# Six PSUM tiles of one bank in place of three tiles of two banks, for the sums of w_down and of the embedding's gate

## The chip, the core and the metric

The kernel runs on one core of one Trainium2 chip. The metric is the device time of one execution in microseconds (us), the median of several runs. TensorE multiplies matrices into PSUM, VectorE, ScalarE and GpSimd do the elementwise work, and SyncE issues the transfers.

## What is computed

One layer of a streaming encoder for 1024 prompt rows and 128 decoding rows (1152 together), model width 1024. Two mixers (sparse attention, gated delta rule) and a merge come first; the change lies in what follows them:

```python
h2 = _rmsnorm(x, norm_ffn)
u_gate, u_val = jnp.split(h2 @ w_up, [D_FF], axis=-1)        # D_FF = 2816
...
act = jax.nn.gelu(_causal_dwconv(ext_f, conv_ffn), approximate=True)
x = x + (act * u_val) @ w_down

gate_p = jax.nn.sigmoid(_rmsnorm(x, norm_ple) @ w_ple_gate)
x = x + gate_p * (p @ w_ple)
...
y = _rmsnorm(x, norm_final)
```

All of it is in float32 and everything is kept transposed: 128 channels on the partitions, rows of x along the free dimension.

## The kernel before

**Products.** Each operand is split into a high part and a low rest (`H`, `L` for activations, `wh`, `wl` for weights; ScalarE casts the high part, VectorE or GpSimd subtracts it for the rest). A product of two 128-wide pieces is three matmuls into one PSUM sum: `wh` with `H`, `wh` with `L`, `wl` with `H`. A weight tile that lies in the buffer `T3` is named `T3H` in the trace, whether high or low.

**The stretch at issue.** The 1152 rows are three blocks `b` of 384. For each block the kernel computes w_down, then the embedding's gate, for eight output tiles `d` of 128 channels. A sum of w_down runs over 22 pieces. It is made in three parts of 8, 8 and 6 pieces, for four `d` at a time (all four first parts, then the second, then the last), so four sums are open at once and they finish one after the other at the end of the group. A sum of the gate runs over 8 pieces in one go. A sum has 384 float32 columns and takes one PSUM bank of 512.

**Evacuation.** When a sum is complete, `evac_down` has VectorE read it out of PSUM, multiplied by the norm's factors (`gt<-up,R` in the trace), add it to the residual (`B<-B,gt`), and form the gate's operand for this `d` (ScalarE `H`, VectorE `L`). `evac_pg` reads the gate's sum in the same way (`gt<-up,R`), then applies the tanh on ScalarE (`gt<-gt`) and adds the result to the residual. A bank is given back to the list of free ones after the read.

**The banks.** Before w_down come the products of w_up, whose sums are two banks wide: three tiles `up0`, `up1`, `up2` of [128, 2, 512]. Two more banks (`rp`) serve the norms. In the last products of w_up, `more_accs` takes each of the three tiles when it comes free and hands its two halves on, as the places of sums of w_down and the gate:

```python
self.accs = _Views([x[:, i, :BW] for x in self.ups.views for i in range(2)])
```

The place that has been free longest is taken first. So two sums that follow each other mostly lie in the two halves of one tile.

**The order.** The order of each engine's instructions is fixed when the program is built: a driver runs the threads of the kernel (products, evacuations, loads, weights) against a small table of costs and issues each instruction as its turn comes. The waits between engines are then put in by the framework, from the tiles that the instructions read and write. Each engine works its list off in order.

Of the kernel before, what the change touches and what calls it, by code (L numbers as in the profile page):

```python
# [7 lines left out]
F32 = mybir.dt.float32  # L8
# [8 lines left out]
PSUM = bass.MemoryType.PSUM  # L17
# [4 lines left out]
NB, BW = 3, 384  # L22
# [65 lines left out]
class _Driver:  # L88
# [23 lines left out]
    def set(self, ev):  # L112
        ev.t = self.cur.t
# [178 lines left out]
class _Kernel:  # L292
# [105 lines left out]

    def more_accs(self):

        for _ in range(3):
            x = yield self.ups
            i = 2 * next(i for i in range(3) if self.ups.views[i] is x)
            self.accs.free += [(self.drv.cur.t, i), (self.drv.cur.t, i + 1)]

    def landed(self, j, t):
        self.drv.cur.dma = t
# [2440 lines left out]
    def merge_ffn(self):  # L2848
        drv, tc = self.drv, self.tc
        base = ExitStack()  # L2850
        self.rp = self.pool(base, "rms")
        self.rpb = _Banks(self.pool(base, "rpp", space=PSUM, side="right"), [128, 512], "rp", 2)
        self.ssq = self.rp.tile([128, T], F32, name="ssq")
        self.R2 = self.rp.tile([128, T], F32, name="R2")
        self.xs = _Banks(self.rp, [128, BW], "xs", 4)
        self.sqs = _Banks(self.rp, [128, BW], "sqs", 2)
        mix = ExitStack()
        mp = self.pool(mix, "mix")
        self.MH = mp.tile([128, KD, T], F32R, name="MH")
        self.ML = mp.tile([128, KD, T], F32R, name="ML")  # L2860
        with ExitStack() as st:
            self.tgs = _Banks(self.pool(st, "tg"), [128, BW], "tg", 6)
            drv.run(drv.spawn(self.dense(self.ja), 9), self.jbd)
        self.sh.close()
        self.evst.close()
        self.acc0.free = []
        h2 = ExitStack()
        self.hp = hp = self.pool(h2, "h2", side="right")
        q = lambda n: hp.tile([128, 4, 2, 288], F32R, name=n)
        self.B1H, self.B1L = q("B1H"), q("B1L")  # L2870
        self.B2 = hp.tile([128, 2, 4, 2, 576], F32R, name="B2")
        self.B2H, self.B2L = self.B2[:, 0], self.B2[:, 1]

        self.TR = {t: hp.tile([128, 4, 2, 288], F32, name="T%d" % t) for t in (0, 2, 3)}
        self.TH, self.TL = {1: q("T1H")}, {1: q("T1L")}
        self.hev2.t = 0.0
        up0, up1 = ExitStack(), ExitStack()
        p = self.pool(up0, "up0", space=PSUM, side="right")
        self.ups = _Views([p.tile([128, 2, 512], F32, name="up0"), None, None])
        self.ups.free = self.ups.free[:1]  # L2880
        drv.spawn(self.dense(self.jo), 9)
        drv.spawn(self.dense(self.ju), 9, self.jo[-1].done)
        drv.run(self.jo[-1].done)
        mix.close()
        t13 = ExitStack()
        p = self.pool(t13, "t13")
        for t in (2, 0, 3):
            self.TH[t] = p.tile([128, 4, 2, 288], F32R, name="T%dH" % t)
        self.TL[2] = p.tile([128, 4, 2, 288], F32R, name="T2L")
        with ExitStack() as st:  # L2890
            self.fp = fp = self.pool(st, "ff")
            self.exts = _Banks(fp, [128, 1026 + 144], "fe", 2)
            self.cs = _Views([])
            self.vs = _Banks(fp, [128, T], "fv", 2)
            self.fev.t = 0.0
            for n, t in enumerate((2, 0, 3)):
                drv.spawn(self.up_parts(t), 1 + n)
            drv.run(*self.aout)
            self.pst.close()
            p = self.pool(up1, "up", space=PSUM)  # L2900
            for i in (1, 2):
                self.ups.views[i] = p.tile([128, 2, 512], F32, name="up%d" % i)
                self.ups.free.append((0.0, i))
            self.accs = _Views([x[:, i, :BW] for x in self.ups.views for i in range(2)])
            self.accs.free = []
            ends = drv.spawn(self.dense(self.jd), 9, self.ju[21].done[S4Y])
            drv.spawn(self.down_loads(), 1)
            for i in range(4):
                drv.spawn(self.load_up(0, range(i, 22, 4)), 1)
            drv.run(self.ast[21])  # L2910
        with ExitStack() as st:
            self.plev.t = 0.0
            self.wp2 = p = self.pool(st, "pl")
            self.gts = _Banks(p, [128, BW], "gt", 4)
            self.pps = _Banks(p, [128, BW], "pp", 4)
            t = self.hp.tile([128, 6, BW], F32, name="T3")
            self.araws = _Views([t[:, i] for i in range(6)])
            self.ends = []
            for b in (1, 2):
                for i in range(6):  # L2920
                    drv.spawn(self.load_up(b, range(i, 22, 6)), 2)
            drv.run(ends)
            drv.run(*self.ends)
        t13.close()
        h2.close()
        up1.close()
        up0.close()
        base.close()


# [106 lines left out]
```

## Time and profile before

| | us |
|---|---|
| median of 3 runs | 2154.72 |
| lowest and highest run | 2152.86, 2160.5 |
| the profiled execution | 2153.31 |
| its span, first to last instruction | 2151.5 |
| TensorE busy in the span | 2065.3 (96%) |
| VectorE busy | 1543.1 (72%) |
| ScalarE busy | 1001.0 (47%) |
| GpSimd busy | 838.2 (39%) |

The profile is of one execution. Its own time stands beside the runs, and its span leaves out what lies before the first and behind the last instruction. A busy time is the time in which at least one instruction of the engine is on record; matmuls overlap in it, and their ends are modelled. Every operation is recorded by one helper, so all rows have the line L192, and groups are told apart by their tiles: `up` is the tile of sums, `gt` the result of its read, `R` the norm's factors.

### The profile page before, as it was taken

The page shows a single profiled execution, that of the slowest core. Times are in us where ns is not written, and L with a number is a line of the kernel's source. Part 1 is how long each engine was busy: PE and PEld are TensorE (multiplying, and loading weights), DVE is VectorE, ACT ScalarE, POOL GpSimd, SP SyncE. Part 2 cuts the span into 40 slices and gives each one's busy share as a digit, 9 for nine tenths or more (in the row PEclk, how much of TensorE's full clock was granted, in tenths as well). Part 3 has the DMA queues.
Part 4 walks back from the last instruction along what each step waited for, and adds up shares of the span by engine and source line. Part 5 has one row for each costly group of instructions (what it writes and reads, how often), then busy time and mean ns, then how long its engine had stood idle before and what let it go on. Part 6 is the DMA issues. An engine that isn't in the chain of part 4 may idle for free.

```text
span 2151.5 us, 37608 instructions
## 1 busy us (share of the span) xinstructions
PE 2065.3 (96%) x13146; PEld 2005.0 (93%) x13146; DVE 1543.1 (72%) x3585; ACT 1001.0 (47%) x1979; POOL 838.2 (39%) x1028
## 2 busy tenths in 40 slices
PE   7999998989999999999999999999999999999997
PEld 6899988989999989999999999999999989999996
DVE  7268988888747787774354778887888866857645
ACT  5267666565535566665133433333333344335332
POOL 5344543423334444454364445565655401101101
PEclk9999999989999999999999999999999999999998
DMA  5444267676555755457764423334443486655542
GB/s 195 119 125 106 80 183 184 158 195 191 165 175 165 218 159 169 140 156 233 238 197 150 128 40 86 73 72 75 78 84 66 93 218 197 192 166 190 168 138 83
DMA packets 318156, 314.56 MB, mean 146 GB/s; under 512 B 117436, under 2 KB 277008, under 8 KB 317840
## 3 DMA queue, kind: packets, MB, share of 16 engines
q1 hardware_dynamic: 317968, 312.17, 52.2%
q8 instruction: 104, 1.70, 0.3%
q14 instruction: 84, 0.69, 0.1%
HBM read 224.91 MB, written 88.81 MB: 146 GB/s over the span
## 4 chain that ended last, share of the span: by engine, by line
PE 56%; DVE 4%; DMA 4%; issue 1%; ACT 1%; POOL 1%; SPq 1%; DVEq 0%; ACTq 0%; POOLq 0%
PE up L192 38%; PE acc L192 12%; PE at L192 6%; PE rp L192 1%; SPq L192 1%; DVE B L192 1%; DVE gt L192 1%; DVE wl L192 1%; DMA evo<-gates 1%; DMA T<-in_w_down 0%; POOL tg L192 0%; POOL wl L192 0%; DVE z L192 0%; DMA obT<-sg 0%; DMA x<-qkv 0%
## 5 line engine op out<-in xcount | busy, mean ns | idle before, releaser
L192 PE MATMUL acc<-H,wh 128*128 128x384 f32 (+2 forms) x1344 | 475.6, 354 | 6.9 <-DVE evo L192 2.1
L192 PE MATMUL acc<-L,wh 128*128 128x384 f32 (+2 forms) x1344 | 456.6, 340 | 1.8 <-POOL L L192 1.3
L192 PE MATMUL acc<-H,wl 128*128 128x384 f32 (+2 forms) x1344 | 456.6, 340 | 1.4 <-POOL wl L192 1.4
L192 POOL TENSOR_TENSOR wl<-wr,wh 128x256 fp32r<-128x256 f32 (+1 forms) x288 | 232.5, 830 | 302.0 <-ACT wh L192 285.8
L192 PEld LDWEIGHTS acc<-H,wh 128*128 128x128 f32 (+1 forms) x1344 | 253.5, 189 | 15.8 <-DVE evo L192 2.4
L192 PEld LDWEIGHTS acc<-L,wh 128*128 128x128 f32 (+1 forms) x1344 | 253.8, 189 | 6.9 <-POOL L L192 2.0
L192 PEld LDWEIGHTS acc<-H,wl 128*128 128x128 f32 (+1 forms) x1344 | 253.4, 189 | 3.6 <-POOL wl L192 2.4
L192 POOL TENSOR_TENSOR ssq<-ssq,sqs 128x384 f32<-128x384 f32 x62 | 67.9, 1094 | 406.5 <-ACT sqs L192 406.4
L192 ACT CAST wh<-wr 128x1024 fp32r<-128x1024 f32 (+3 forms) x140 | 122.5, 883 | 148.6 <-PE up L192 54.7
L192 POOL TENSOR_TENSOR wl<-s,wh 128x256 fp32r<-128x256 f32 x104 | 98.4, 964 | 145.3 <-ACT wh L192 145.3
L192 PE MATMUL up<-B,wh 128*128 128x288 f32 x704 | 143.2, 297 | 3.5 <-DVE B L192 2.8
L192 DVE SCALAR_TENSOR_TENSOR T<-fe,cwf,T 128x512 f32<-128x512 f32 x132 | 124.6, 944 | 17.8 <-ACT T L192 16.4
L192 PE MATMUL up<-T,wh 128*128 128x288 f32 (+1 forms) x416 | 125.6, 302 | 2.2 <-DVE T L192 2.2
L192 PEld LDWEIGHTS up<-B,wh 128*128 128x128 f32 x704 | 113.5, 189 | 3.9 <-DVE B L192 3.1
L192 ACT ACTIVATE ja<-SC,cola 128x768 bf16<-128x768 f32 (+2 forms) x93 | 96.7, 1039 | 37.1 <-DVE cola L192 26.8
L192 ACT CAST wh<-s 128x512 fp32r<-128x512 f32 x88 | 52.5, 620 | 122.0 <-PE up L192 122.0
L192 PE MATMUL up<-B,wl 128*128 128x288 f32 x352 | 104.4, 297 | 0.0
L192 DVE TENSOR_TENSOR wl<-wr,wh 128x512 fp32r<-128x512 f32 (+1 forms) x87 | 72.5, 849 | 29.6 <-ACT wh L192 29.6
L192 PE MATMUL up<-T2H,wh 128*128 128x288 f32 (+1 forms) x272 | 85.1, 313 | 6.4 <-DVE gt L192 3.4
L192 PE MATMUL up<-T1H,wh 128*128 128x288 f32 (+1 forms) x272 | 85.6, 315 | 0.0
L192 PE MATMUL up<-T2L,wh 128*128 128x288 f32 (+1 forms) x272 | 84.6, 311 | 0.9 <-DVE T2L L192 0.9
L192 PE MATMUL up<-T1L,wh 128*128 128x288 f32 (+1 forms) x272 | 85.1, 313 | 0.0
(483 smaller groups left out, 5991.7 us busy)
## 6 DMA issues: line engine op xcount, KB each, us to landing
wr<-in_w_in SPq DMA_DIRECT2D x48, 512.0 KB, 4.3
AT<-fv SPq DMA_DIRECT2D x22, 576.0 KB, 5.5
wr<-in_w_down SPq DMA_DIRECT2D x24, 512.0 KB, 4.2
T<-in_w_down SPq DMA_DIRECT2D x24, 512.0 KB, 3.5
wr<-in_w_up SPq DMA_DIRECT2D x22, 512.0 KB, 10.7
gates<-evo SPq DMA_DIRECT2D x48, 192.0 KB, 1.9
T<-AT SPq DMA_DIRECT2D x44, 192.0 KB, 3.8
qkv<-evo SPq DMA_DIRECT2D x36, 192.0 KB, 4.1
```

What stands on the lines that cost most here:

```text
L192: r = f(*a, **k)
```

## The change

`more_accs` no longer hands on the halves of the old tiles. When both `up1` and `up2` have come free, their pool is closed and a new one is opened with four tiles `dn0` to `dn3` of one bank each; when `up0` is free, its pool is closed for one with `dn4` and `dn5`. The sums take these six tiles as they took the six halves. Nothing else is edited.

```diff
     def more_accs(self):
 
+        got = set()
         for _ in range(3):
             x = yield self.ups
-            i = 2 * next(i for i in range(3) if self.ups.views[i] is x)
-            self.accs.free += [(self.drv.cur.t, i), (self.drv.cur.t, i + 1)]
+            got.add(next(i for i in range(3) if self.ups.views[i] is x))
+            for old, new, own, n, k in ((self.up1, self.dn1, {1, 2}, 4, {}), (self.up0, self.dn0, {0}, 2, dict(side="right"))):
+                if own <= got:
+                    old.close()
+                    got -= own
+                    p = self.pool(new, "dn%d" % n, space=PSUM, **k)
+                    for _ in range(n):
+                        i = len(self.accs.views)
+                        self.accs.views.append(p.tile([128, 512], F32, name="dn%d" % i)[:, :BW])
+                        self.accs.free.append((self.drv.cur.t, i))
...
-        up0, up1 = ExitStack(), ExitStack()
-        p = self.pool(up0, "up0", space=PSUM, side="right")
+        self.up0, self.up1, self.dn0, self.dn1 = [ExitStack() for _ in range(4)]
+        p = self.pool(self.up0, "up0", space=PSUM, side="right")
...
-            p = self.pool(up1, "up", space=PSUM)
+            p = self.pool(self.up1, "up", space=PSUM)
...
-            self.accs = _Views([x[:, i, :BW] for x in self.ups.views for i in range(2)])
-            self.accs.free = []
+            self.accs = _Views([])
...
-        up1.close()
-        up0.close()
+        self.dn1.close()
+        self.dn0.close()
```

On every engine the same instructions stand in the same order before and after, tile names aside. The waits differ, on TensorE above all. Two places follow; in brackets stands which engine's semaphore a matmul waits for (`Activation` is ScalarE).

The first place is TensorE in w_down of the first block: the last three matmuls of the sum for `d` = 0 and the first of the last part of the sum for `d` = 1, which lies in the other half of `up1`. Before:

```order
L192 MATMUL up1_14468<-T0H_14413,T3H_14414 128x384 [waits Activation_49]
L192 MATMUL up1_14468<-T2_14550,T3H_14414 128x384 [waits DVE_49]
L192 MATMUL up1_14468<-T0H_14413,T3H_14414 128x384
L192 MATMUL up1_14468<-T2H_14412,wh_20095 128x384 [waits DVE_49,Activation_49]
L192 MATMUL up1_14468<-T2L_14415,wh_20095 128x384
L192 MATMUL up1_14468<-T2H_14412,wl_20096 128x384
```

And with the change:

```order
L192 MATMUL dn0_19799<-T0H_14413,T3H_14414 128x384 [waits Activation_49]
L192 MATMUL dn0_19799<-T2_14550,T3H_14414 128x384 [waits DVE_49]
L192 MATMUL dn0_19799<-T0H_14413,T3H_14414 128x384
L192 MATMUL dn1_19800<-T2H_14412,wh_20109 128x384 [waits Activation_49]
L192 MATMUL dn1_19800<-T2L_14415,wh_20109 128x384
L192 MATMUL dn1_19800<-T2H_14412,wl_20110 128x384 [waits DVE_49]
```

The first matmul of the second sum waited for VectorE's read `gt` of the first sum, and for ScalarE's cast of its own `wh` from the buffer `wr2`; now it waits for the cast alone. The wait for `wl`, which VectorE makes before that read, stands on the matmul that uses it.

The second place is TensorE in the first block's gate: the end of one sum and the first half of the next. The read of the first sum is issued when twelve matmuls of the second have been issued. Before:

```order
L192 MATMUL up1_14468<-H3_20150,wl_20745 128x384
L192 MATMUL up1_14468<-H3_20150,T3H_14414 128x384 [waits Activation_49]
L192 MATMUL up1_14468<-L3_20151,T3H_14414 128x384
L192 MATMUL up1_14468<-H3_20150,T3H_14414 128x384 x2
...
L192 MATMUL up1_14468<-H3_20150,T3H_14414 128x384
L192 MATMUL up1_14468<-H3_20150,T3H_14414 128x384 [waits DVE_49]
L192 MATMUL up1_14468<-L3_20151,T3H_14414 128x384
```

And with the change:

```order
L192 MATMUL dn0_19799<-H3_20164,wl_20759 128x384
L192 MATMUL dn1_19800<-H3_20164,T3H_14414 128x384 [waits Activation_49]
L192 MATMUL dn1_19800<-L3_20165,T3H_14414 128x384
L192 MATMUL dn1_19800<-H3_20164,T3H_14414 128x384 [waits DVE_49]
...
L192 MATMUL dn1_19800<-H3_20164,T3H_14414 128x384 x2
L192 MATMUL dn1_19800<-L3_20165,T3H_14414 128x384
L192 MATMUL dn1_19800<-H3_20164,T3H_14414 128x384 [waits DVE_49]
```

Before, the thirteenth matmul of the second sum waited for the read, and the read for the twelfth. With the change both waits of the second sum are for low halves of its weight tile, and the read waits for the last matmul of its own sum.

## Rows read from the trace of the kernel before

**Rows 1.** The page: TensorE's busy time, and its granted clock in 40 slices.
```profile
PE 2065.3 (96%) x13146; PEld 2005.0 (93%) x13146; DVE 1543.1 (72%) x3585; ACT 1001.0 (47%) x1979; POOL 838.2 (39%) x1028
PEclk9999999989999999999999999999999999999998
```
**Rows 2.** Busy time by stretch; behind POOL the granted clock, DMA share, GB/s.
```profile
core 0: us, PE busy (x) PEld busy (x) DVE busy (x) ACT busy (x) POOL busy (x), PEclk, DMA share, GB/s
1680.00:1724.00 44.00, 44.00 (x332) 44.00 (x331) 37.81 (x57) 19.22 (x33) 18.82 (x20) 1.00 0.47 89
...
1755.00:2136.00 381.00, 361.37 (x2056) 353.65 (x2054) 244.12 (x442) 155.76 (x233) 45.17 (x41) 1.00 0.53 166
```
**Rows 3.** Waits of TensorE from 1755 us on: us in total, times, longest.
```profile
PE up L192 <- DVE gt L192: 12.0, 15, 1.4
PE up L192 <- ACT wh L192: 3.0, 4, 0.7
...
PE up L192 <- ACT T3H L192: 1.5, 2, 0.7
PE up L192 <- DVE L L192: 1.4, 3, 0.6
```
**Rows 4.** Timeline of TensorE, first block's gate: start us, us, instruction [idle before].
```profile
1840.28 0.34 PE L192 MATMUL up<-H,wl 128*128 128x384 f32 x1
1841.27 0.44 PE L192 MATMUL up<-H,wh 128*128 128x384 f32 x1 [0.65 <-DVE gt L192]
1841.56 0.33 PE L192 MATMUL up<-L,wh 128*128 128x384 f32 x1
```
**Rows 5.** Timeline of VectorE at the same place.
```profile
1840.66 0.56 DVE L192 TENSOR_TENSOR gt<-up,R 128x384 f32<-128x384 f32 x1 [0.75 <-PE up L192]
```
**Rows 6.** Timeline of TensorE, first block's w_down.
```profile
1762.26 0.34 PE L192 MATMUL up<-T0H,T3H 128*128 128x384 f32 x1
1763.34 0.41 PE L192 MATMUL up<-T2H,wh 128*128 128x384 f32 x1 [0.74 <-ACT T3H L192]
1763.59 0.33 PE L192 MATMUL up<-T2L,wh 128*128 128x384 f32 x1
```
**Rows 7.** Timeline of VectorE at the same place.
```profile
1762.63 0.56 DVE L192 TENSOR_TENSOR gt<-up,R 128x384 f32<-128x384 f32 x1 [0.47 <-PE up L192]
```
**Rows 8.** Timeline of ScalarE at the same place.
```profile
1759.34 0.83 ACT L192 CAST wh<-wr 128x768 fp32r<-128x768 f32 x1
```
**Rows 9.** Timeline of TensorE, first block, first sum of the gate.
```profile
1822.81 0.33 PE L192 MATMUL up<-L,wh 128*128 128x384 f32 x1
1822.98 0.33 PE L192 MATMUL up<-H,wl 128*128 128x384 f32 x1
1823.15 0.33 PE L192 MATMUL up<-H,wh 128*128 128x384 f32 x1
```
**Rows 10.** Timeline of TensorE, first block's w_down, two sums on.
```profile
1769.53 0.34 PE L192 MATMUL up<-T0H,wl 128*128 128x384 f32 x1
1771.24 0.41 PE L192 MATMUL up<-T2H,T3H 128*128 128x384 f32 x1 [1.38 <-DVE gt L192]
```
**Rows 11.** Timeline of VectorE at the same place.
```profile
1770.55 0.54 DVE L192 TENSOR_TENSOR gt<-up,R 128x384 f32<-128x384 f32 x1
```
**Rows 12.** Busy time in the stretch around the end of the first block's w_down.
```profile
1819.30:1827.20 7.90, 6.70 (x38) 6.38 (x38) 7.81 (x12) 5.20 (x11) 2.22 (x2) 1.00 0.33 103
```
**Rows 13.** Timeline of VectorE in that stretch.
```profile
1819.30 0.56 DVE L192 TENSOR_TENSOR gt<-up,R 128x384 f32<-128x384 f32 x1 [0.88 <-PE up L192]
...
1822.97 0.55 DVE L192 TENSOR_TENSOR gt<-up,R 128x384 f32<-128x384 f32 x1
...
1826.54 0.61 DVE L192 SCALAR_TENSOR_TENSOR L<-B,nrm,H 128x384 fp32r<-128x384 f32 x1
```
**Rows 14.** Timeline of TensorE from the seventh sum's end.
```profile
1818.39 0.34 PE L192 MATMUL up<-T0H,wl 128*128 128x384 f32 x1
...
1826.27 0.34 PE L192 MATMUL up<-H,wh 128*128 128x384 f32 x1
1827.20 0.44 PE L192 MATMUL up<-L,wh 128*128 128x384 f32 x1 [0.59 <-DVE L L192]
```
**Rows 15.** The reads of sums: duration ns min/median/max, first and last start us.
```profile
L192 DVE TENSOR_TENSOR gt<-up,R x48: 543/557/558, 1762.6 to 2134.4; 128x384 f32<-128x384 f32 x48
```

## The prediction

> **What bounds the kernel now.** I read the page first. TensorE is busy for 96% of the span and its granted clock stands at full speed in nearly every slice [rows 1], so whatever takes time from TensorE takes it from the kernel. The diff touches only the products of w_down and of the embedding's gate, so the next view is that stretch, 1755 to 2136 us: TensorE is busy 361.4 of 381.0 us there, VectorE 244.1, ScalarE 155.8, the DMA engines 53% [rows 2]. TensorE is the bound, with 19.6 us idle. Then the waits of TensorE in that stretch: 15 waits for VectorE's `gt`, 12.0 us together; 4 for ScalarE's `wh` and 2 for its `T3H`, 4.5 us; 3 for VectorE's `L`, 1.4 us [rows 3].
>
> `gt<-up,R` is VectorE's read of a finished sum out of PSUM. One of these waits, in order of time: TensorE starts the matmul before at 1840.28, the next at 1841.27 and the one behind it at 1841.56 [rows 4]. VectorE starts its read at 1840.66, for 0.56 us, and it ends just ahead of the late matmul [rows 5]. So TensorE stands still for the length of one read and the two handovers around it.
>
> The six waits put down to ScalarE are of the same kind. In the first, TensorE starts matmuls at 1762.26, 1763.34 and 1763.59 [rows 6]; a read runs from 1762.63 to 1763.19 [rows 7]; the cast that this matmul needs (`wh<-wr`, by the first place shown in the order of instructions) had ended at 1759.34 + 0.83 = 1760.17 [rows 8]. The view named the cast of a later weight tile. That makes 21 waits.
>
> **The change, part by part.** Nothing is added to the work: on all five engines the same instructions stand in the same order, tile names aside. What differs is who waits for whom. Before, two sums share a tile `up`, and the order of instructions makes the tile as a whole pass from hand to hand, though the sums lie in different banks: a matmul for the second sum that is issued behind the read of the first waits for that read. 21 matmuls have that wait before and not after, which is the count above: four in each block's w_down, three in each block's gate. In 11 of the pairs the read stands 3 to 21 matmuls deep in the second sum and before waits for those as well; after, it waits for its own sum alone.
>
> What one stall costs is the distance of matmul starts, because the ends of matmuls are modelled. Without a stall they start 0.17 to 0.18 us apart (1822.81, 1822.98 in [rows 9]); I take 0.175, so 0.35 for two steps.
> - Read deep in the next sum: 1841.56 - 1840.28 = 1.28, less 0.35 = 0.93 us [rows 4]. There are 11 of these (listed with 0.65 us idle).
> - Read right behind its sum: 1763.59 - 1762.26 = 1.33, less 0.35 = 0.98 us [rows 6]. There are 7 (listed with 0.74; six of them under ScalarE).
> - The same with VectorE still busy when the sum is ready: 1771.24 - 1769.53 = 1.71 [rows 10], plus a second step of 0.25 as in [rows 6], less 0.35 = 1.61 us. There are 3. The read itself runs 1770.55 to 1771.09 [rows 11].
>
> As a check on the counts: 11 x 0.65 + 3 x 1.38 + 0.74 = 12.0, the sum of the `gt` row in [rows 3], and six of 0.74 are 4.4 against the 4.5 of its ScalarE rows. The sum: 11 x 0.93 + 7 x 0.98 + 3 x 1.61 = 21.9 us.
>
> What is late next? All waits that stay are for weights and for the next operand. The matmul of [rows 6] would be due at 1762.26 + 0.175 = 1762.44, and its weights were there at 1760.17 [rows 8], 2.3 us earlier. The casts of later weights start when TensorE has finished an earlier weight tile, so they move forward with it. The waits that the change writes out anew, for the low halves of weights, stood before too, implied by the wait for the read, which VectorE does later than those. I cost them at nothing. No transfer is waited for either: TensorE has none in [rows 3], and the DMA engines are busy 53% [rows 2].
>
> One place gives something back: the end of w_down in each block, where the gate's last eighth of operand, `L`, comes out of the last sum's read. VectorE is busy 7.81 of 7.90 us there [rows 12], from the read of the seventh sum at 1819.30 to the end of `L` at 1826.54 + 0.61 = 1827.15 [rows 13]; 7.85 us that TensorE's speed doesn't shorten. TensorE's last matmul of that sum starts at 1818.39 [rows 14]. After, the read can start 0.38 us behind it (1840.66 - 1840.28 in [rows 4] and [rows 5]), at 1818.77, and `L` ends at 1826.62. The matmul that needs it is the 41st behind 1818.39 and would be due at 1818.39 + 41 x 0.175 = 1825.57; it waits 1.1 us, plus 0.1 for the restart. Before, it lost 1827.20 - 1826.27 - 0.175 = 0.76 [rows 14] and the same 0.1. So 0.4 us more is lost, three times: 1.2 us. Bounds for that: nothing, and the whole stall removed just ahead, 3 x 0.93 = 2.8.
>
> Reading a bank beside matmuls that write another isn't new: the 48 reads last 543 to 558 ns whether TensorE stands or runs [rows 15], and beside the read at 1822.97 [rows 13] the matmuls keep their step [rows 9]. I cost it at nothing.
>
> Gain: 21.9 - 1.2 = 20.7 us. The profiled execution took 2153.3 us, 1.8 of it around the span of 2151.5; less 20.7 is 2132.6. The median of the three runs is 1.4 above the profiled one, so I forecast 2134.
>
> **The rivals.**
> *VectorE takes over in w_down.* It is as good as full for 7.9 us at a block change [rows 12], and one stall of w_down was 1.71 long because it was busy. If all twelve waits of w_down only changed their name, each block would keep 0.98 + 1.61 + 0.98 + 0.93 = 4.5 us, 13.5 in all, and 8.4 would be gained: 2146. Against it: VectorE is busy 64% of the stretch [rows 2]. Chance 8%.
>
> *No change.* The waits could stand for real ones, for a bank that is used again, or another wait could be waiting behind each. Then the time stays at 2153 to 2155. For it: the sums lay in six banks before already. Against it: a stall comes while the second half is written and the read is of the first, and the operands were early. Chance 5%. The Trainium skill speaks for this one (Perfetto Trace Analysis, Matmuls): "Independent matmul groups should rotate through different PSUM banks so the ACT/DVE evacuation of one overlaps the next group's matmuls". By that rule the kernel before was in order and nothing would be gained; the trace disagrees, as its evacuation does not overlap, by [rows 4] and [rows 5].
>
> *Slower.* Since no engine's order changes and the waits only get fewer, it can end later only if instructions take longer. The place is the matmuls that now run beside a read. The gain is used up if the step grows by 20.7 / 2160 = 10 ns over the 2160 matmuls of both products (8 x 3 sums of 22 x 3 and 8 x 3 of 8 x 3), to 0.185 us; by 20 ns it ends 22 us slower, near 2177. Against it: the steps in [rows 9], and a stretch of 44 us with TensorE 100% busy that keeps the full clock [rows 2]. Chance 3%. The Trainium skill (PSUM — Partial Sum Buffer, PSUM bank collisions raise a hardware error) says that two engines on different banks ran clean; by that rule this rival has no price, and the trace agrees.
>
> **How the numbers follow.** The forecast has 84%. Its own ends: 21.9 gained with no offset for the median is 2131.4, and the runs of before reach 1.9 below their median, so 2129; at the top, half of the gain lost is 2153.3 - 10.4 + 1.4 = 2144. The other three cases hold 16%, so the range may end there. 0.5% of the median is 10.8 us, about what a measurement can tell from no change: faster means under 2143.9. That is the forecast and a part of the first rival, 87%; within 0.5% 10%; slower 3%.
>
> **What would show it.** Right: TensorE's row of waits for `gt` is gone, and the `wh` and `T3H` rows with it; the stretch is some 20 us shorter with about 4 us idle; reads start 0.4 us behind their own sum; the waits for `L` grow from 0.6 to about 1 us. Wrong: the same number of waits under another name (`wl`, `wh`, `L`), the step of matmuls above 0.18 us, or reads longer than 0.56 us. A lower granted clock in the stretch, or weights that land late, would also break it.

## The result, and the profile after

| | before | after |
|---|---|---|
| median of 6 runs, us | 2154.61 | 2139.44 |
| lowest and highest run | 2152.86, 2162.33 | 2132.81, 2142.96 |
| the profiled execution | 2153.31 | 2132.81 |
| its span | 2151.5 | 2131.0 |

The ratio is 0.9918 (95% interval 0.9896 to 0.994). Run again beside other kernels, with 6 runs of it and 11 of the kernel before, the changed kernel gave 0.9908 (0.9887 to 0.9929). Of the ten executions of the kernel with a tile of four banks (below), one took 3386 us at a granted clock of 0.555 and is left out of its ratio. The forecast was 2134 us, a ratio of 0.9904. The two profiled executions lie 20.5 us apart; the forecast for that was 20.7.

The page of the changed kernel, its span and its first section, beside [rows 1]:

```profile
span 2131.0 us, 37597 instructions
...
PE 2060.1 (97%) x13146; PEld 2001.8 (94%) x13146; DVE 1541.9 (72%) x3585; ACT 1000.0 (47%) x1979; POOL 842.6 (40%) x1028
```

The number of matmuls is the same; the span has lost 20.5 us, TensorE's busy time 5.2. The stretch of the two products, to the end of its matmuls, beside [rows 2]:

```profile
1755.00:2115.50 360.50, 356.82 (x2055) 354.39 (x2053) 243.74 (x441) 154.25 (x233) 47.81 (x41) 1.00 0.55 176
```

The idle time of TensorE is 3.7 us of 360.5 us here; before it was 19.6 of 381.0. Its waits from 1745 us on, beside [rows 3] (us in total, times, longest):

```profile
PE rp L192 <- ACT sqs L192: 2.7, 1, 2.7
PE rp L192 <- DVE rr_r L192: 2.4, 1, 2.4
PE dn L192 <- DVE L L192: 1.5, 3, 0.6
PE dn L192 <- ACT H L192: 1.1, 3, 0.5
PE dn L192 <- DVE T2L L192: 0.9, 1, 0.9
PE rp L192 <- POOL ssq L192: 0.8, 1, 0.8
```

The row for `gt` is gone, and the rows for `wh` and `T3H` with it: what they named was never ScalarE. (`dn` is what `up` was.) `H`, one wait of 0.2 us before, is larger and `ssq` is new; the experiments come to them. The place of [rows 6] and [rows 7], TensorE and then VectorE:

```profile
1762.05 0.34 PE L192 MATMUL dn<-T0H,T3H 128*128 128x384 f32 x1
1762.23 0.34 PE L192 MATMUL dn<-T2H,wh 128*128 128x384 f32 x1
1762.40 0.33 PE L192 MATMUL dn<-T2L,wh 128*128 128x384 f32 x1
1762.58 0.33 PE L192 MATMUL dn<-T2H,wl 128*128 128x384 f32 x1
```

```profile
1762.43 0.56 DVE L192 TENSOR_TENSOR gt<-dn,R 128x384 f32<-128x384 f32 x1
```

The read runs from 1762.43 to 1762.99 and the matmuls of the next sum keep their step of 0.17 to 0.18 us beside it. The read itself has not become longer (min/median/max in ns, beside [rows 15]):

```profile
L192 DVE TENSOR_TENSOR gt<-dn,R x48: 543/551/559, 1762.4 to 2114.8; 128x384 f32<-128x384 f32 x48
```

**One measure for all runs.** The time from the start of the first to the start of the last of the 2160 matmuls of both products, read from the timeline, is free of what happens elsewhere: 1722.99 to 2134.00, 411.0 us, before, and 1722.73 to 2114.46, 391.7 us, after. It is "the stretch" in what follows. Two executions of the changed kernel gave 391.7 and 391.8, though one began the stretch 7.1 us later.

### The profile page after: what moved, and what is told of

Its sections match the earlier page's. It is cut to its first block, busy times and chain, and to the rows that moved or that the text cites. A ratio compares the mean times of both kernels' runs of the same rounds, so it can differ in the third digit from the quotient of the medians.

```text
span 2131.0 us, 37597 instructions
## 1 busy us (share of the span) xinstructions
PE 2060.1 (97%) x13146; PEld 2001.8 (94%) x13146; DVE 1541.9 (72%) x3585; ACT 1000.0 (47%) x1979; POOL 842.6 (40%) x1028
## 4 chain that ended last, share of the span: by engine, by line
PE 56%; DMA 4%; DVE 3%; POOL 1%; issue 1%; ACT 1%; SPq 1%; DVEq 0%; POOLq 0%; ACTq 0%
PE up L192 23%; PE dn L192 15%; PE acc L192 11%; PE at L192 7%; DMA evo<-gates 1%; DMA xs<-AT 1%; POOL tg L192 1%; PE rp L192 1%; DMA r<-gsc 1%; SPq L192 1%; DVE B L192 1%; DVE wl L192 0%; POOL wl L192 0%; DMA tg<-gates 0%; DMA evo<-vTs 0%
## 5 line engine op out<-in xcount | busy, mean ns | idle before, releaser
L192 PE MATMUL up<-T,wh 128*128 128x288 f32 x352 | 104.2, 296 | 2.2 <-DVE T L192 2.2
L192 POOL TENSOR_TENSOR cvc<-cvc,evo 128x384 f32<-128x384 f32 (+2 forms) x48 | 43.8, 913 | 79.9 <-ACT evo L192 58.1
L192 DVE TENSOR_SCALAR_CACHE_REDUCE e<-half,colv 128x384 bf16<-128x384 int16 (+5 forms) x96 | 71.1, 740 | 0.9
L192 PEld LDWEIGHTS up<-T,wh 128*128 128x128 f32 x352 | 66.6, 189 | 2.8 <-DVE T L192 2.8
L192 ACT ACTIVATE z<-z,mx 128x256 f32<-128x256 f32 (+7 forms) x79 | 59.6, 759 | 16.9 <-DVE mx L192 16.8
```

The lines of the kernel that those rows point to most:

```text
L192: r = f(*a, **k)
```

## The experiments

The theory: the 21 stalls come from two sums in one tile, which the order of work treats as one thing, and each costs what it was sized at. Rivals: the gain has to do with the pools being made anew, or with which banks are used; or the stalls hide other waits.

**1. New pools, tiles of two banks.** The changed kernel with the pools opened as in the change, but with two sums in each tile:

```
-                    for _ in range(n):
+                    for _ in range(n // 2):
...
+                        x = p.tile([128, 2, 512], F32, name="dn%d" % i)
+                        self.accs.views += [x[:, 0, :BW], x[:, 1, :BW]]
```

> The pools are closed and opened anew as in the change, but with three tiles of two banks. The order of every engine is that of before, and 21 matmuls wait for a read of the other half, as before. Theory (the waits come from the shared tile): the time of before, a ratio of 1.000 within 0.003, TensorE's row of waits for gt about 12 us. Rival (the new pools, or the place of the sums, make the gain): the time of the change, a ratio near 0.991, no such row.

Ratio to before 1.0007 (0.999 to 1.0025); the stretch 411.0 us. Its waits are those of [rows 3], to the tenth:

```profile
PE dn L192 <- DVE gt L192: 12.0, 15, 1.4
PE dn L192 <- ACT wh L192: 3.0, 4, 0.7
...
PE dn L192 <- ACT T3H L192: 1.5, 2, 0.7
```

So of what the change edits it is the size of the tiles that matters: not the pools, not the moment at which banks are handed on.

**2. Old tiles, halves handed out in turn.** The kernel before, with the halves handed on so that sums that follow each other lie in different tiles where possible (`LATE` holds the sixth place back for 60 us of the driver's time):

```
-            self.accs = _Views([x[:, i, :BW] for x in self.ups.views for i in range(2)])
+            self.accs = _Views([self.ups.views[n][:, i, :BW] for n, i in ((1, 0), (2, 0), (1, 1), (2, 1), (0, 0), (0, 1))])
...
+LATE = 60.0
...
+                self.accs.free += [(t, 4), (t + LATE, 5)]
```

> The tiles of before, two banks each, but their halves are handed on in turn, so that two sums that follow each other lie in different tiles. 23 matmuls still wait for a read of the other half of their tile, but the read belongs to a sum one or more sums back, at least 15 matmuls or 2.6 us earlier. Theory (a stall is the length of read and handover, and only where the read comes right before): nearly all of the gain, a ratio of 0.990 to 0.993, TensorE's waits for gt under 3 us. Rival (each wait costs whatever its distance, or only one-bank tiles help): the time of before, 12 us or more of waits for gt.

Ratio 0.9929 (0.9907 to 0.9952), the stretch 395.1 us. The waits for the shared tile are still there in the order, 23 of them, but in most the read is over when the other half's matmul comes; six cost time:

```profile
PE up L193 <- DVE gt L193: 4.0, 6, 0.7
```

The ratio is within what was expected; the 4.0 us are more than the 3 that they were to stay under. One of the six, TensorE and then VectorE:

```profile
1858.31 0.34 PE L193 MATMUL up<-B1H,T3H 128*128 128x384 f32 x1
1859.30 0.44 PE L193 MATMUL up<-B1H,T3H 128*128 128x384 f32 x1 [0.65 <-DVE gt L193]
```

```profile
1858.68 0.56 DVE L193 TENSOR_TENSOR gt<-up,R 128x384 f32<-128x384 f32 x1 [1.23 <-PE up L193]
```

It is the stall of [rows 4] and [rows 5] again, with the same 0.99 us between two starts. So the order in which places are handed out can avoid most of the stalls without one-bank tiles, but not all.

**3 and 4. Part of the change, and more than undoing it.** Four sums in tiles of their own and two in a shared one (the first two lines); and one tile of four banks beside one of two (the last line):

```
+                    if n == 2:
+                        x = p.tile([128, 2, 512], F32, name="dn%d" % i)
...
+                    x = p.tile([128, n, 512], F32, name="dn%d" % i)
```

> Four of the six sums' places are tiles of one bank, the last two share a tile as before. 7 of the 21 waits are left, in the trace of before 4 of 0.98, 2 or 3 of 0.92 and 1 of 1.61 us of lost time, 7.3 us in all. Theory (the gain is the sum of the stalls): 14.6 us less at most, 13 to 14 after what the block changes give back, a profiled time near 2140 and a ratio near 0.994; the row of waits for gt at 4 to 5 us. Rival (VectorE becomes the bound and caps the gain): as fast as the whole change.

> The opposite direction: four of the six places share one tile of four banks, the other two a tile of two. The order is the same, 31 matmuls wait for a read in place of 21. Theory: the ten further waits cost about 0.95 us each where the read comes right before, so 5 to 10 us more than before, 2158 to 2163, a ratio of 1.002 to 1.005. Rival (the stalls are waits for VectorE's queue, whichever tile): no change against before.

Ratios 0.9938 (0.9916 to 0.996) and 1.0023 (1.0008 to 1.0037), both as expected. With four of six the stretch lost 14.8 us, a little more than the 14.6 that were to be the most. In the four-bank kernel 9 of the ten further waits cost time. The waits, of the first and then of the second:

```profile
PE dn L192 <- DVE gt L192: 4.1, 5, 1.4
...
PE dn L192 <- ACT T3H L192: 0.7, 1, 0.7
PE dn L192 <- ACT wh L192: 0.7, 1, 0.7
```

```profile
PE dn L192 <- DVE gt L192: 17.5, 24, 1.4
PE dn L192 <- ACT wh L192: 3.0, 4, 0.7
...
PE dn L192 <- ACT T3H L192: 1.5, 2, 0.7
```

All five kernels up to here have the same instructions in the same order as before; only who shares a tile differs:

| | stalls at shared tiles | the stretch, us |
|---|---|---|
| the change | 0 | 391.7 |
| halves in turn | 6 | 395.1 |
| four of six | 5 + 1 + 1 = 7 | 396.2 |
| before, and new pools with old tiles | 15 + 4 + 2 = 21 | 411.0 |
| a tile of four | 24 + 4 + 2 = 30 | 418.3 |

From 0 to 21 stalls it is (411.0 - 391.7) / 21 = 0.92 us each, from 21 to 30 (418.3 - 411.0) / 9 = 0.81. These are net of what comes back elsewhere, and so the first few stalls seem cheaper: the kernels with 6 and 7 lie only 0.57 and 0.64 us a stall above the change. By the starts of the matmuls the three block changes together lose 1.8 us with 30 stalls, 2.3 with 21, 2.8 with 7, 3.1 with 6 and 3.9 with none, and of these kernels only the one with none waits for `ssq` (1.0 us). So the stalls make the effect, and a smaller wait does stand behind them. The rival by which nothing would be gained has fallen.

**5. What is given back at a block change.** The prediction let TensorE lose 0.4 us more at each of three places. In the changed kernel the waits there are in part others than before: three for ScalarE's `H` in place of one, and one for GpSimd's sum of squares, `ssq`. The first idea was that VectorE's splits of the gate's next weight tiles stand in the way. Two variants move them behind the block's last `L`; the second also starts the norm one weight tile later. The changed kernel ran again beside them.

```
+        if j.after is not None:
+            yield j.after
...
+                if d in (1, 2):
+                    self.jd[-1].after = self.gev[7][b]
...
-                drv.spawn(self.rms(b, cols, self.Re[4][b]), 1)
+                drv.spawn(self.rms(b, cols, self.Re[4][b]), 1, self.gate1[b].done)
```

The last two lines are of the second variant alone. In both, the driver laid other instructions out anew as well: the order of ScalarE's casts changed, and so did the place of the norm in TensorE's list.

> The changed kernel once more, beside two variants of it, in more rounds. If the gain is the 20 us of stalls that the two traces show, the ratio to the kernel before lies near 0.990 to 0.992, and the stretch from the first to the last 384-column matmul is 391 to 392 us long again, with no wait of TensorE for the sums' readers but those at the three block changes (about 0.27 + 0.64 us each). If part of the first comparison's gain was a matter of which chip it ran on, the ratio comes nearer to 1 (0.994 or more) with the same stretch.

> The changed kernel, but VectorE's splits of the gate's second and third weight tile are issued behind the block's last L instead of between the sums' reads; the norm's matmuls thereby come some 12 matmuls earlier. Theory: what is left of waiting at a block change comes from VectorE's queue, which is still busy with splits and L's when the last sums want their reader. Then TensorE's waits for H and L at the three block changes fall from 2.6 us to under 1 us. The matmuls of the norm, issued earlier, meet GpSimd's sum of squares: the wait for it, 0.8 us in the change, may grow to 3 or 6 us in all, so that the stretch of 391.7 us comes out between 390 and 396. Rival: the waits at the block change come from the length of the chain H, L, read itself, whatever lies beside it on VectorE; then they stay at 2.4 to 2.8 us.

> As the run with the splits behind the last L, and the norm's chain is started behind the gate's second weight tile, so that its matmuls come some 12 matmuls later than in the change. Theory (VectorE's queue, and the norm's matmuls too early for GpSimd's sum): waits for H and L under 1 us, none over 0.3 us for GpSimd's sum of squares, and the stretch 388 to 390 us instead of 391.7; ratio to the kernel before 0.988 to 0.991. Rival (the chain itself): H and L as in the change, 2.4 to 2.8 us, and the stretch 391 to 392. If the norm's factor, later now, is wanted by the gate's read before it is ready, a wait for it appears instead, and the stretch is longer than 392.

Ratios 0.9908 (0.9887 to 0.9929), 0.9896 (0.9875 to 0.9916) and 0.9914 (0.9892 to 0.9936), which don't tell the three apart; the stretches are 391.8, 391.3 and 390.5 us. The waits, of the first variant and then of the second:

```profile
PE rp L192 <- POOL ssq L192: 1.7, 2, 0.8
...
PE dn L192 <- DVE L L192: 0.4, 2, 0.2
```

```profile
PE rp L192 <- DVE rr_r L192: 4.1, 3, 2.4
...
PE dn L192 <- DVE L L192: 0.4, 2, 0.2
```

The waits for `H` and `L` fell from 2.6 to 0.4 us (by the starts of the matmuls, the loss at the block changes from 3.9 to 1.5), so what VectorE has to do ahead of them sets them. But the time came back at the norm: in the first its matmuls wait twice for GpSimd, in the second the norm's factor `rr_r` is late (one such wait of 2.4 us stands in every run; the two others are new). Half a hit: the waits for `H` and `L` fell as expected, but the first variant's wait for `ssq` is 1.7 us instead of 3 to 6, and the second's stretch missed its 388 to 390. With other orders changed beside the splits, these two runs don't say what holds VectorE up; the next run goes behind it.

**6. What fills VectorE there.** The changed kernel at its first block change, VectorE, GpSimd and TensorE:

```profile
1812.52 1.15 DVE L192 TENSOR_TENSOR T1L<-T,T1H 128x384 fp32r<-128x384 f32 x1
...
1815.36 0.55 DVE L192 TENSOR_TENSOR gt<-dn,R 128x384 f32<-128x384 f32 x1
...
1816.42 0.55 DVE L192 TENSOR_TENSOR B<-B,gt 128x384 f32<-128x384 f32 x1
1816.89 1.51 DVE L192 TENSOR_TENSOR wl<-wr,wh 128x512 fp32r<-128x512 f32 x1
...
1819.32 0.68 DVE L192 TENSOR_TENSOR wl<-wr,wh 128x512 fp32r<-128x512 f32 x1
1819.92 1.38 DVE L192 TENSOR_TENSOR B<-B,gt 128x384 f32<-128x384 f32 x1
...
1822.42 0.61 DVE L192 SCALAR_TENSOR_TENSOR L<-B,nrm,H 128x384 fp32r<-128x384 f32 x1
```

```profile
1812.23 1.02 POOL L192 TENSOR_TENSOR ssq<-ssq,sqs 128x384 f32<-128x384 f32 x1 [33.62 <-ACT sqs L192]
1816.70 1.14 POOL L192 TENSOR_TENSOR ssq<-ssq,sqs 128x384 f32<-128x384 f32 x1 [3.46 <-ACT sqs L192]
1819.61 1.27 POOL L192 TENSOR_TENSOR ssq<-ssq,sqs 128x384 f32<-128x384 f32 x1 [1.76 <-ACT sqs L192]
1823.78 2.71 POOL L192 TENSOR_TENSOR ssq<-ssq,sqs 128x384 f32<-128x384 f32 x1 [2.90 <-ACT sqs L192]
```

```profile
1814.62 0.34 PE L192 MATMUL dn<-T0H,wl 128*128 128x384 f32 x1
...
1822.00 0.44 PE L192 MATMUL dn<-H,wh 128*128 128x384 f32 x1 [0.27 <-ACT H L192]
1823.08 0.45 PE L192 MATMUL dn<-L,wh 128*128 128x384 f32 x1 [0.64 <-DVE L L192]
...
1826.55 0.83 PE L192 MATMUL rp<-ones,ssq 128*128 128x1 f32 x6 [0.76 <-POOL ssq L192]
```

What to look at is one kind of instruction on VectorE that has two lengths. `B<-B,gt` takes 0.55 at 1816.42 and 1.38 at 1819.92; `wl<-wr,wh` takes 0.68 and 1.51. Each long one began while an add of GpSimd was running, and ended 0.4 to 0.6 us after it: the adds end at 1817.84 and 1820.88, the two instructions at 1818.40 and 1821.30. So VectorE stood for about 0.83 us each time, twice on the way to the last `L`. The same happens a third time ahead of the seventh sum's read: `T1L<-T,T1H`, which takes 0.54 to 0.55 us in 10 of its 12 cases, takes 1.15 at 1812.52, beside the add that ends at 1813.25. Over the whole change, 4 of the 24 `B<-B,gt` start while an add is running and take 1.37 to 1.38 us; the other 20 take 0.55 to 0.56. To test it, GpSimd's adds behind the fifth to eighth output tile were cut to 8 columns, with everything else left as and where it was, so the norm's factor leaves out most of the squares of these tiles:

```
-            nc.gpsimd.tensor_add(ssq, ssq, s)
+            n = 8 if step == 4 and d >= 4 else BW
+            nc.gpsimd.eng.tensor_add(ssq[:, :n], ssq[:, :n], s[:, :n])
+            drv.note(POOL, 0.1 + BW * 2.3e-3, True)
```

> The changed kernel with the same instructions in the same order, but GpSimd's adds to the sum of squares behind the fourth to eighth output tile of w_down are of 8 columns instead of 384 (so the norm's factor leaves out most of those tiles' squares). In the change two of VectorE's instructions at each block change take 1.4 to 1.5 us instead of 0.55 to 0.68, each from the time at which one of these adds of GpSimd runs (VectorE's B<-B,gt at 1819.92 ends 0.42 us behind GpSimd's add, which runs 1819.61 to 1820.88). Theory: GpSimd's add holds VectorE up by 0.8 us twice per block change, and that, not VectorE's own work, is why TensorE waits for H and L. Then B<-B,gt lasts 0.55 us again at 1820, the waits for H and L fall from 2.6 us to under 0.5, the wait for GpSimd's sum (0.8) goes too, and the stretch is 386.5 to 388.5 us instead of 391.7. Rival: VectorE's own splits and L's set it; then both instructions stay long or become short without effect, H and L stay at 2.0 to 2.7 us, and only the 0.8 us go: 390.5 to 391.5 us.

Ratio 0.9886 (0.9856 to 0.9916); the stretch 386.3 us, 5.4 less than the change. VectorE, GpSimd, and the waits from 1745 us on:

```profile
1823.82 0.56 DVE L192 TENSOR_TENSOR gt<-dn,R 128x384 f32<-128x384 f32 x1 [0.16 <-PE dn L192]
...
1828.03 0.55 DVE L192 TENSOR_TENSOR B<-B,gt 128x384 f32<-128x384 f32 x1
1828.49 0.69 DVE L192 TENSOR_TENSOR wl<-wr,wh 128x512 fp32r<-128x512 f32 x1
```

```profile
1825.30 0.20 POOL L2513 TENSOR_TENSOR ssq<-ssq,sqs 128x8 f32<-128x8 f32 x1 [4.04 <-ACT sqs L192]
1828.43 0.20 POOL L2513 TENSOR_TENSOR ssq<-ssq,sqs 128x8 f32<-128x8 f32 x1 [2.93 <-ACT sqs L192]
```

```profile
PE rp L192 <- ACT sqs L192: 2.7, 1, 2.7
PE rp L192 <- DVE rr_r L192: 2.4, 1, 2.4
PE dn L192 <- DVE T2L L192: 0.9, 1, 0.9
```

`H`, `L` and `ssq` are gone from the waits altogether, a little further than expected (for `ssq` the add's own length is enough). The seventh sum's read (1823.82) starts 0.38 us behind the last matmul of its sum, as it does in the other two blocks, and from it to the end of the last `L` it is 6.50 us, where the change took 7.67. The order of all instructions is that of the change, so GpSimd's adds are the cause of the whole loss at the block changes.

**7. A version with the whole computation.** The last three adds of each block are given to VectorE, which needs 0.47 us of its queue for one where GpSimd held it up for 0.83:

```
-            yield POOL
-            nc.gpsimd.tensor_add(ssq, ssq, s)
+            late = step == 4 and d >= 5
+            yield DVE if late else POOL
+            (nc.vector if late else nc.gpsimd).tensor_add(ssq, ssq, s)
```

> The changed kernel with the whole computation, but the adds to the sum of squares behind the sixth to eighth output tile of w_down are done by VectorE (one more instruction of 0.47 us step each) instead of by GpSimd. Two of them stand ahead of the last L of a block. If GpSimd's adds held VectorE up by 0.8 us each at that place, VectorE gets 2 x (0.8 - 0.5) = 0.7 us of it back per block, the waits for H and L fall from 2.6 us to between 0.3 and 1.8 us, the wait of 0.8 us for GpSimd's sum goes, and the stretch is 388 to 390.5 us instead of 391.7. The matmuls of the norm stand some places earlier in TensorE's list, so a wait for VectorE's last add may take the place of the one for GpSimd. If VectorE's own work alone counts, the waits for H and L grow to 4 us or more and the stretch to 393 or more.

Ratio 0.9897 (0.9877 to 0.9917), median 2133.49 us; the stretch 387.3 us, the shortest with the whole computation, 4.4 under the change. It went further than expected: no wait for `H`, `L` or `ssq` is left. Part of it may be the order: one split of a weight tile, 0.6 us of VectorE's time, now comes behind the last `L`, and this run doesn't tell the two apart. The change itself did not run beside it, and the intervals of the ratios overlap (0.9908 and 0.9897), so the gain over the change is read from the stretch alone.

## Why the prediction was right, point by point

- **TensorE bounds the stretch, and the stalls are its idle time.** Right. Taking them away shortened the stretch by nearly all that they cost.
- **21 waits, six of them under ScalarE's name.** Right: six rows' worth of `wh` and `T3H` went with the 15 of `gt`, and came back with them when the tile was two banks wide again.
- **21.9 us for them.** Right: by the starts of the matmuls, the 21 places together lose 21.9 us before and nothing after, 1.04 a stall.
- **What is late next: nothing but the block changes.** Nearly. No weight became late by the change (each trace has one wait of 0.67 us for a weight in the first 10 us of the stretch, ahead of every stall, in another place). But the norm's matmuls, issued just behind a block change, did: with TensorE ahead of where it was, in the first block they wait 0.76 us for GpSimd's sum (1826.55 in the timeline shown, behind the add at 1823.78 that took 2.71 us). In all they take 1.0 us more of the stretch, which the prediction had not looked at.
- **1.2 us given back at the block changes.** This term was mis-sized. By the starts of the matmuls for `H` and `L`, a block change loses 0.43 + 0.91 = 1.34 us in each of the first two blocks and 1.19 in the third, 3.9 us; before, 0.75, 0.74 and 0.85, 2.3 us. That is 1.5 us given back, 0.6 in each of the first two blocks and 0.3 in the third. With the norm's 1.0 it is 2.5, between the 1.2 taken and the upper bound of 2.8. The step behind it: the read of the seventh sum was to start 0.38 us behind the last matmul of its sum. In the third block it does; in the first it started 1815.36 - 1814.62 = 0.74 us behind it, and 0.75 in the second, since VectorE was still busy with the sixth tile's `L`, which the add at 1812.23 had put off: in the run that cuts this add the read starts 0.38 us behind in all three blocks, in the run of experiment 7, which leaves it to GpSimd, 0.75 in the first. The other part of that step held: from that read to the end of the last `L` it was to take 7.85 us whatever TensorE does, and it took 1823.03 - 1815.36 = 7.67. But the prediction read [rows 12] as VectorE's own work, and two of the instructions in it were long by 0.83 us each, for GpSimd's adds (before, too: in that stretch one `B<-B,gt` took 1.37 us and one `wl<-wr,wh` 1.51). With short adds the same way takes 6.50 us. Nor did the loss show as a longer wait for `L`, as the prediction had it: that row stayed at 0.6 us at most, and a wait for ScalarE's `H`, which comes out of the same chain, stood in front of it. Of the first rival, by which w_down's waits only change their name and 13.5 us stay, these 1.5 us are all that came.
- **The sum.** 21.9 - 1.5 - 1.0 = 19.4 us in the stretch, and it lost 19.3 (411.0 - 391.7). The remaining 1.2 of the 20.5 us lie outside: 0.3 in its earlier start, and 1.0 in the tail, where ten small matmuls of the last norm ran at half clock before and at full clock after. The agreement of 20.5 with 20.7 is thus partly luck: 1.4 us less in the stretch, 1.2 more elsewhere.
- **The offset from the profiled execution to the median, 1.4.** It was 6.6 for the changed kernel, whose profiled execution was the lowest of its six. That, and no stall, is why the median is 5.4 above the forecast. The profile of the second run of the change shows where: set against the first, it falls from 1.3 to 6.5 us behind between 394 and 466 us, 7.1 us behind by 1300 us, and from there to the end no more than 0.1 is added. The two executions, 400 to 600 us, the first and then the second (the clock is the third number from the right):

```profile
400.00:600.00 200.00, 192.68 (x1231) 181.78 (x1230) 169.41 (x624) 116.47 (x235) 62.26 (x85) 0.97 0.65 177
```

```profile
400.00:600.00 200.00, 192.30 (x1190) 180.84 (x1189) 165.84 (x620) 116.06 (x236) 60.30 (x84) 0.95 0.63 176
```

- **Longer instructions beside a read.** They didn't come: the step of undisturbed matmuls is 0.1747 us before and 0.1746 after, over some 2100 of them, and the reads' median went from 557 to 551 ns. That two banks can be used side by side without an error, which the prediction cites, says nothing yet of the time; these numbers do.

## What to carry to other kernels

Look at what a wait is for, not only at whose name it has: here a bank was free, and the tile around it was not. Things that different engines use at different times deserve tiles of their own, since an order of work that is kept by tile makes neighbours in a tile wait for each other, at the price of one read and two handovers (0.9 to 1.6 us here) a time. And when a queue is full, compare the lengths of equal instructions in it before calling it work: the long ones were waiting.

## What the runs showed of the hardware

An add on GpSimd with operands in SBUF holds up VectorE's instructions with two operands there: `B<-B,gt` 1.38 us instead of 0.55, and it works the other way too: GpSimd's own add took 2.71 us (2.91 in the second run of the change) instead of 1.04 (the median of 62) while VectorE was busy without a gap until 1825.64, and ended 0.85 us after that. The Trainium skill (SBUF — State Buffer, SBUF: two separate sides) says that the two share a pair of ports that one of them takes for a whole instruction while the other is blocked; this trace agrees. VectorE's reads of sums out of PSUM (`gt<-dn,R`, one operand in each memory) stayed between 543 and 559 ns in all 48 cases, also in the two that started while an add was running.

The granted clock of the last matmuls differed between two runs of the same instructions. The ten matmuls of the last norm, before and then after (windows; the clock is again the third number from the right):

```profile
2137.00:2139.50 2.50, 2.16 (x10) 2.16 (x10) 0.00 (x0) 0.29 (x1) 0.00 (x0) 0.50 0.00 0
```

```profile
2117.00:2119.10 2.10, 1.27 (x10) 1.19 (x10) 0.14 (x1) 0.52 (x1) 0.00 (x0) 1.00 0.00 0
```

At the lower level (0.50, 1.2 GHz) they were busy for 2.16 us, at full clock (2.4 GHz) for 1.27. TensorE had stood still for 2.9 us ahead of them before, for 2.7 after. From the last matmul of the stretch to the end it was 17.5 us before and 16.5 after, and 16.5 to 17.6 in the other runs; what decides it stays open. It is not the length of that standstill alone: with four of six it was 2.9 us as before, and the ten were busy for 1.28 us; in the first variant with later splits it was 2.7 us as after, and they were busy for 2.30 at 0.50.
